# Seven-product groups that add up in one PSUM bank, the last product put off, and the third gate chunk by seven

## The chip, the cores and the metric

The kernel runs on one core of a Trainium2 chip. The metric is the time of one launch on the device in microseconds. The engines are TensorE (PE, matmuls; PEld are its weight loads), VectorE (DVE), ScalarE (ACT), GpSimd (POOL) and SyncE (SP), which issues the weight loads from HBM.

## The reference

A decoder trunk of two layers in float32 with 512 tokens and width 1024. Each layer is a half-step FFN, a mixer and a second half-step FFN; the first mixer is gated linear attention (GLA), the second is stick-breaking attention.

```python
def swiglu(h, w_gate, w_up, w_down):
    return (jax.nn.silu(h @ w_gate) * (h @ w_up)) @ w_down        # hidden width 2816

# GLA: chunks of 64, 4 heads, a decay by channel
log_a = jax.nn.log_sigmoid(gk_lr @ w_gk2 + b_gk) / 16
state = exp(b_last) * state + einsum(k * exp(b_last - b), v)      # b = cumsum(log_a)
o = rmsnorm(o, o_norm) * jax.nn.silu(g)

# stick-breaking: 16 heads of 64, blocks of 128 queries, mask: key before query
sp = where(mask, softplus(z), 0)
rem = cumsum(sp, reverse=True) - sp
weights = where(mask, exp(log_sigmoid(z) - rem), 0)

for i in range(2):
    x = x + 0.5 * swiglu(rmsnorm(x, ffn1_norm[i]), ...)
    x = x + mixer_i(rmsnorm(x, mix_norm[i]))
    x = x + 0.5 * swiglu(rmsnorm(x, ffn2_norm[i]), ...)
return rmsnorm(x, final_norm)
```

## The kernel before

Everything stays on chip but the weights. The residual is eight tiles `xs` of 128 features by 512 tokens. Each float32 operand is cut into a high and a low part (ACT writes the high one, L135 for weights, and DVE the rest, L136), and each product is three matmuls: high by high, low by high, high by low.

**FFN.** The hidden width is cut into 11 chunks of 256 columns, in six groups (`GROUPS`). Gate and up of a chunk are computed either as two features of 128 columns by `feat` (24 matmuls of 512 tokens each, PSUM tile `ps_f`, L64), or by `seven`: one 2×2 block product in the Strassen–Winograd form, seven products of 12 matmuls of 256 columns (L545) in place of eight, with sums of weight blocks (`s12`, `s34`) and of input blocks (`t_half`) on one side and additions of the results on the other. The ups go by `seven` from chunk 2 on, the gates from chunk 3 on (`SEVEN = 3`). The gated hidden tiles (high `hh`, low `hl`) of a group then go into the downs: one `down` accumulates `ps_d` over a group's tiles for some output features and adds into `xs` (L310).

**A group of seven before.** It uses three banks `w`, `z` and `q`, each in two halves. Four products fill or add on in the left halves, three have a half for themselves; five additions on DVE (`add`, L556, and L600) and two copies on ACT (`u2` at L580, `c5` at L587) put the two output tiles `o0` and `o1` together. For a gate, `left` (L560) applies Silu to the half that comes straight from PSUM, and `rest` (L566) applies it in place to what was added in SBUF; for an up the same two multiply by the gate. `rest` also keeps its Silu instruction in `st["silu"]`.

**Order.** Entries (a `feat`, a `down`, half a `seven`) stand in one queue, `feed`. It cuts weights up to three entries ahead and issues loads up to six ahead; raw weights have two buffers, cut weights four. What an engine executes in which order is set by a scheduler of the framework, which works from dependences and its own estimate of durations, and not by the source alone; `tc.issue_after(i)` adds only that an instruction does not come before `i`.

**Activation tables.** ACT holds one set of function tables at a time; ACT_TABLE_LOAD brings another. GLA and stick-breaking need Exp and Ln in turn. Before each of them the kernel asks for the one set that holds both, behind the last Silu it knows of:

```python
def exp_ln_tables(after):                      # L443, called with st["silu"]
    with tc.issue_after(after):
        st["tab"] = nc.scalar.preload_act_table_set("natural_log_exp_and_others").ins

def act(o, i, fn, **kw):                       # L447: every Exp and Ln of the mixers
    with tc.issue_after(st["tab"]):
        st["last"] = nc.scalar.activation(o, i, fn, **kw).ins
```

The last FFN does the same for a set with Sqrt (L716). Where an activation needs a set that is not the loaded one, the compiler puts a load ahead of it. `act` is what L450 is in the rows of the profile (L452 in the changed kernel).

**Stick-breaking.** Sixteen heads run as eight pairs. For each block of queries ACT makes the logits' parts `l` and `r` from PSUM (L1201, L1207), then Exp and Ln of `l` (L450), DVE adds, PE sums along the keys (`ps_T`), and ACT takes Exp of that for the weights `wt`. The projections of later heads run on PE in between.

Of the kernel before, what the change touches and what calls it, by code (L numbers as in the profile page):

```python
# [19 lines left out]
P = 128  # L20
# [12 lines left out]
def decoder(ctx: ExitStack, tc: tile.TileContext, a: dict, out: bass.AP):  # L33
# [257 lines left out]

                feed.q.append(Entry([u], body))

    def down(w, r0, nf, hs, part, nxt):

        nd = KD // nf
        src = w[r0 : r0 + nf * P, part * nd * P : (part + 1) * nd * P]
        ch = Chunk(src.rearrange("(f p) c -> p f c", p=P), nf, nd * P)
        ch.few = True

        def body(W):
            (wh, wl), = W
            for m in range(nd):
                ps = psum("ps_d")
                s = slice(m * P, (m + 1) * P)
                for f in range(nf):
                    mm3(ps, wh[:, f, s], wl[:, f, s], hs[f][0], hs[f][1], f == 0, f == nf - 1)
                k = part * nd + m
                x = like(xs[k], 4)
                nc.vector.scalar_tensor_tensor(  # L310
                    out=x, in0=back_by(ps, 4), scalar=0.5, in1=x, op0=ALU.mult, op1=ALU.add
                )
                if nxt is not None:
                    nxt(k)
                yield

        feed.q.append(Entry([(ch, lambda t: t, nf, nd * P)], body))
# [135 lines left out]
    class FFN:  # L453
# [4 lines left out]


        GROUPS = ((0, 2), (2, 4), (4, 6), (6, 8), (8, 9), (9, 11))  # L460
        NORMED, SEVEN = 6, 3
        SEVEN_UP = (2, 3, 4, 5, 6, 7, 8, 9, 10)

        def __init__(self, wg, wu, wd, gi, nxt, first=False, last=False):
            self.gi, self.normed, self.first = gi, False, first
            self.evac_g_, self.evac_u_ = self.evac_g, lambda ps: self.evac_u(ps, 0)
            if first:
                self.NORMED = 8
            self.defer, self.gates = [], []
            self.lead = []  # L470
            self.hs = [[] for _ in self.GROUPS]
            base, downs = len(feed.q), []
            self.base = base
            self.sums_by = 10**6
            for group, (c0, c1) in enumerate(self.GROUPS):
                slots, put = 2 * (c1 - c0), 0
                for i in range(slots):
                    c, f = c0 + i // 2, i % 2
                    if f == 0:
                        g, u = Chunk(cols(wg, c * 256, 256), KD, 256), Chunk(cols(wu, c * 256, 256), KD, 256)  # L480
                    d = self.defer if i == 0 and c == 0 else None
                    f_ = f
                    if first and c == 0:

                        g, u = (Chunk(cols(w, f * P, P), KD, P) for w in (wg, wu))
                        self.lead += [g, u]
                        f_ = 0
                    if c >= self.SEVEN:
                        if f == 0:
                            self.seven(g)  # L490
                    elif c not in self.SEVEN_UP:
                        feat(g, f_, self.evac_g, defer=self.defer if first and i == 1 else d, o=quads, m=four)
                    elif f == 0:
                        feat(g, 0, self.evac_g, o=quads, m=four), feat(g, 1, self.evac_g, o=quads, m=four)
                    if c not in self.SEVEN_UP:
                        feat(u, f_, lambda ps, h=group: self.evac_u(ps, h), defer=d, o=quads, m=four)
                    elif f == 1:
                        while c < self.SEVEN and put < len(downs) // 2:
                            down(*downs[put])
                            put += 1  # L500
                        self.sums_by = min(self.sums_by, len(feed.q) - base)
                        self.seven(u, group)

                    while c >= self.SEVEN and put < len(downs) * (i + 1) // slots:
                        down(*downs[put])
                        put += 1
                for x in downs[put:]:
                    down(*x)
                n = 2 * (c1 - c0)
                end = group + 1 == len(self.GROUPS)  # L510
                downs = [(wd, c0 * 256, n, self.hs[group], part, nxt if end else None) for part in range(n)]
            self.count = len(feed.q) - base
            if last:
                back_tok(wd, c0 * 256, n, self.hs[group], nxt)
            else:
                for x in downs:
                    down(*x)
            self.total = len(feed.q) - base

        def seven(self, ch, group=None):  # L520
# [43 lines left out]
            def rest(o, c):  # L564
# [4 lines left out]
                nc.vector.tensor_tensor(out=o[:, c:T], in0=o[:, c:T], in1=self.gates.pop(0)[:, c:T], op=ALU.mult)  # L569
                self.close(o, group)  # L570

            def body_1(W):
                ax, s = W

                v["w"], v["z"], v["q"] = psum("ps_w"), psum("ps_z"), psum("ps_q")
                w, z, q = (v[n][:, 0:H] for n in "wzq")
                v["o"] = self.tp.tile([P, T], F32, tag="t", name="o0")
                prod(w, ax, 0, half(0, 0))
                v["u2"] = part("u2")
                nc.scalar.copy(v["u2"], w)  # L580
                yield
                prod(z, s, 4, lambda j: self.t_half(1, j))
                add(v["u2"], z, v["u2"])
                yield
                prod(q, s, 0, lambda j: self.t_half(0, j))
                v["c5"] = part("c5")
                nc.scalar.copy(v["c5"], q)  # L587
                yield
                prod(w, ax, 4, half(4, 0), first=False)
                left(v["o"], w)  # L590
                yield

            def body_2(W):
                s, a22 = W
                q, y = v["q"][:, 0:H], v["z"][:, H:T]
                o0, o1 = v["o"], self.tp.tile([P, T], F32, tag="t", name="o1")
                prod(y, s, 0, lambda j: self.t_half(2, j))
                u3 = o1[:, 0:H]
                add(u3, y, v["u2"])
                nc.vector.tensor_tensor(out=o1[:, H:T], in0=u3, in1=v["c5"], op=ALU.add)  # L600
                yield
                prod(q, s, 4, half(4, 1), first=False)
                add(o0[:, H:T], q, v["u2"])
                rest(o0, H)
                yield
                o = v["w"][:, H:T]
                prod(o, a22, 0, lambda j: self.t_half(3, j))
                add(o1[:, 0:H], o, u3)
                rest(o1, 0)
                yield  # L610


            feed.q.append(Entry([(ch, lambda t: t[:, :, 0:P], KD, P), (ch, sums_12, KD, P)], body_1))
            feed.q.append(Entry([(ch, sums_34, KD, P), (ch, lambda t: t[:, 4:8, P:], 4, P)], body_2))

        def t_half(self, i, j):

# [71 lines left out]
        def run(self, between=None):  # L689
            with tc.tile_pool(name="hp", bufs=8, reuse_waits="tile") as self.hp, tc.tile_pool(  # L690
                name="tp", bufs=5, reuse_waits="tile"
            ) as self.tp:
                st["few"] = self.hp
                new_norm()

                if self.first:
                    with tc.manual_schedule():
                        feed.entries(1)
                        stats_b(turned=True)
                        flush(self.defer)  # L700
                else:
                    two_halves(stats_a)
                    stats_b(turned=True)
                    flush(self.defer)
                done = feed.pos - self.base
                for job, n in ((self.normed_input, self.NORMED - done), (self.sums, self.sums_by - self.NORMED)):
                    todo = list(job())
                    for i in range(n):
                        for piece in todo[i * len(todo) // n : (i + 1) * len(todo) // n]:
                            piece()  # L710
                        feed.entries(1)
                    self.normed = True
                    st["h"], st["l"] = zip(*self.n)
                feed.entries(self.count - self.sums_by)
                if between is not None:
                    with tc.issue_after(st["silu"]):  # L716
                        nc.scalar.preload_act_table_set("sqrt_and_others")
                    feed.q[feed.pos].split()
                    between(self.tp)
                feed.entries(self.total - self.count)  # L720
# [844 lines left out]
```

## Time and profile before

| | |
|---|---|
| median of 3 runs | 1797.32 us (1796.83 to 1797.62) |
| profiled execution, its own time | 1798.32 us |
| its span; mean granted clock of TensorE | 1796.5 us; 0.997 |
| PE, DVE, ACT busy | 1771.0, 1450.4, 906.9 us |
| read from HBM | 175.17 MB, 99 GB/s over the span |
| ACT_TABLE_LOAD in the program | 6: at L1395, L445 (twice), L674 (twice), L717 |
| first FFN; GLA; stick-breaking loop | to about 340 us; 340 to 560; 1250.62 to 1412.17 |

The page counts as busy the time in which an engine executes; the granted clock is 1 at full speed. In rows of the chain and of the timeline the first number is the start in us from the span's start and the second the time of the row's instructions together. In square brackets stands how long the engine had sat idle, and which instruction ended that. In groups, `| 28.6, 421 |` is busy us in all and mean ns of one. In rows of windows come the length, then for PE, PEld, DVE, ACT and POOL the busy time with its instructions, then PEclk, DMA share and GB/s.

### The profile page before, as it was taken

The page shows a single profiled execution, that of the slowest core. Times are in us where ns is not written, and L with a number is a line of the kernel's source. Part 1 is how long each engine was busy: PE and PEld are TensorE (multiplying, and loading weights), DVE is VectorE, ACT ScalarE, POOL GpSimd, SP SyncE. Part 2 cuts the span into 40 slices and gives each one's busy share as a digit, 9 for nine tenths or more (in the row PEclk, how much of TensorE's full clock was granted, in tenths as well). Part 3 has the DMA queues.
Part 4 walks back from the last instruction along what each step waited for, and adds up shares of the span by engine and source line. Part 5 has one row for each costly group of instructions (what it writes and reads, how often), then busy time and mean ns, then how long its engine had stood idle before and what let it go on. Part 6 is the DMA issues. An engine that isn't in the chain of part 4 may idle for free.

```text
span 1796.5 us, 30288 instructions
## 1 busy us (share of the span) xinstructions
PE 1771.0 (99%) x12502; PEld 1622.2 (90%) x12502; DVE 1450.4 (81%) x2371; ACT 906.9 (50%) x1428; POOL 9.6 (1%) x23
## 2 busy tenths in 40 slices
PE   9999999999999999999999999999999999999998
PEld 7899999888988899999989999998877888999997
DVE  7988887787868988878898888786777579888785
ACT  6544445455645444444554444454777544544444
POOL 0000000100000000000000000000000000000000
PEclk9999999999999999999999999999999999999999
DMA  6243333321222333333333333322222223333321
GB/s 212 71 133 114 106 118 103 96 72 57 87 71 94 117 106 106 106 113 100 107 111 101 106 106 118 106 83 83 59 71 71 71 94 118 106 106 111 125 83 71
DMA packets 177614, 179.19 MB, mean 100 GB/s; under 512 B 4098, under 2 KB 167988, under 8 KB 177476
## 3 DMA queue, kind: packets, MB, share of 16 engines
q1 hardware_dynamic: 176224, 175.13, 30.4%
q8 instruction: 98, 1.61, 0.4%
q0 software_dynamic: 576, 1.05, 0.2%
q10 hardware_dynamic: 676, 1.07, 0.2%
q14 instruction: 40, 0.33, 0.1%
HBM read 175.17 MB, written 2.10 MB: 99 GB/s over the span
## 4 chain that ended last, share of the span: by engine, by line
PE 84%; DVE 9%; ACT 3%; DMA 3%; issue 1%; SPq 0%; DVEq 0%; ACTq 0%
PE ps_d L64 24%; PE ps_w L545 15%; PE ps_f L64 13%; PE ps_z L545 10%; PE ps_q L545 10%; PE ps_t L64 4%; PE ps_b L64 4%; DVE wl L136 2%; DMA raw<-in_ffn_w_up_dram 2%; DVE l L1211 1%; PE ps_bt L64 1%; ACT wh L135 1%; PE ps_z L1167 1%; DVE r L1219 1%; DMA raw<-in_sb_w_in_dram 1%
## 5 line engine op out<-in xcount | busy, mean ns | idle before, releaser
L136 DVE TENSOR_TENSOR wl<-raw,wh 128x1024 fp32r<-128x1024 f32 x242 | 259.4, 1073 | 72.2 <-ACT wh L135 71.6
L135 ACT CAST wh<-raw 128x1024 fp32r<-128x1024 f32 (+1 forms) x242 | 223.9, 927 | 149.4 <-PE ps_f L64 53.1
L64 PE MATMUL ps_d<-hh,wh 128*128 128x512 f32 x672 | 254.9, 379 | 0.0
L64 PE MATMUL ps_d<-hh,wl 128*128 128x512 f32 x672 | 254.7, 379 | 0.0
L64 PE MATMUL ps_d<-hl,wh 128*128 128x512 f32 x672 | 254.7, 379 | 0.0
L135 ACT CAST wh<-s 128x1024 fp32r<-128x1024 f32 x136 | 142.2, 1046 | 117.0 <-PE ps_q L545 80.3
L136 DVE TENSOR_TENSOR wl<-s,wh 128x1024 fp32r<-128x1024 f32 x136 | 166.0, 1222 | 24.1 <-ACT wh L135 23.0
L64 PE MATMUL ps_f<-xh,wh 128*128 128x512 f32 x464 | 180.7, 390 | 0.3 <-DVE ol L1257 0.2
L64 PE MATMUL ps_f<-xh,wl 128*128 128x512 f32 x464 | 176.9, 381 | 0.5 <-DVE wl L1444 0.4
L64 PE MATMUL ps_f<-xl,wh 128*128 128x512 f32 x464 | 177.0, 381 | 0.0
L310 DVE SCALAR_TENSOR_TENSOR x<-ps_d,x 128x512 f32<-128x512 f32 x184 | 125.2, 689 | 60.9 <-PE ps_d L64 60.7
L545 PE MATMUL ps_z<-th,wh 128*128 128x256 f32 x544 | 150.1, 276 | 0.2 <-DVE u L556 0.2
L545 PE MATMUL ps_w<-nh,wl 128*128 128x256 f32 x544 | 149.6, 275 | 0.0
L545 PE MATMUL ps_w<-nl,wh 128*128 128x256 f32 x544 | 149.6, 275 | 0.0
L545 PE MATMUL ps_z<-th,wl 128*128 128x256 f32 x544 | 149.6, 275 | 0.0
L545 PE MATMUL ps_z<-tl,wh 128*128 128x256 f32 x544 | 149.6, 275 | 0.0
L545 PE MATMUL ps_w<-nh,wh 128*128 128x256 f32 x544 | 149.5, 275 | 0.0
L135 ACT CAST wh<-rawd 128x1024 fp32r<-128x1024 f32 x84 | 88.0, 1048 | 121.5 <-PE ps_d L64 103.2
L64 PEld LDWEIGHTS ps_d<-hl,wh 128*128 128x128 f32 x672 | 127.0, 189 | 18.0
L64 PEld LDWEIGHTS ps_d<-hh,wl 128*128 128x128 f32 x672 | 127.2, 189 | 16.5
L64 PEld LDWEIGHTS ps_d<-hh,wh 128*128 128x128 f32 x672 | 127.2, 189 | 16.5
L136 DVE TENSOR_TENSOR wl<-rawd,wh 128x1024 fp32r<-128x1024 f32 x84 | 102.8, 1224 | 34.5 <-ACT wh L135 34.1
(279 smaller groups left out, 4621.6 us busy)
## 6 DMA issues: line engine op xcount, KB each, us to landing
raw<-in_ffn_w_gate_dram SPq DMA_DIRECT2D x43, 1024.0 KB, 5.2
raw<-in_ffn_w_up_dram SPq DMA_DIRECT2D x43, 1024.0 KB, 5.2
rawd<-in_ffn_w_down_dram SPq DMA_DIRECT2D x84, 512.0 KB, 3.4
raw<-in_gla_w_in_dram SPq DMA_DIRECT2D x12, 1024.0 KB, 5.1
raw<-in_sb_w_in_dram SPq DMA_DIRECT2D x16, 512.0 KB, 3.8
raw<-in_gla_w_out_dram SPq DMA_DIRECT2D x4, 1024.0 KB, 5.0
raw<-in_sb_w_in_dram SPq DMA_DIRECT2D x4, 1024.0 KB, 5.2
raw<-in_sb_w_out_dram SPq DMA_DIRECT2D x4, 1024.0 KB, 4.9
```

The source lines that it names most:

```text
L64: st["pe"] = nc.tensor.matmul(ps, l, r, start=first, stop=last).ins
L135: nc.scalar.copy(h, r).ins,
L136: nc.vector.tensor_tensor(out=l, in0=r, in1=h.bitcast(F32), op=ALU.subtract).ins,
L310: nc.vector.scalar_tensor_tensor(out=x, in0=back_by(ps, 4), scalar=0.5, in1=x, op0=ALU.mult, op1=ALU.add)
L545: nc.tensor.matmul(pairs(o), l_, r_, start=first and j + n == 0, stop=j == 3 and n == 2, skip_group_check=True)
L1167: nc.tensor.matmul(o, l, r, start=first, stop=False, skip_group_check=True)
L1211: nc.vector.tensor_tensor_scan(out=l[:, c][:, ::-1], data0=r[:, c][:, ::-1], data1=l[:, c][:, ::-1], initial=0.0, op0=ALU.add, op1=ALU.add,)
L1219: nc.vector.tensor_tensor(out=r, in0=ps[:, 0:w], in1=l, op=ALU.subtract)
```

## The change

Four things are changed.

- **One bank.** ACT copies `w` into the bank `z` (from PSUM to PSUM), and the product that made `u2` is accumulated on top of it; ACT copies the sum out as `u2`. The product for the right half of `o1` is accumulated on top of that again, and the last product on top of that. DVE's additions fall from five to two per group, ACT's copies rise from two to three.
- **The last product is put off.** It becomes the function `fourth` in the list `self.later`, which `put_off` runs in the third step of the next group of seven, or ahead of a down that needs its tile, or before the last downs. Its `left` and `rest` (for a gate: the Silu of `o1`) go with it.
- **The third gate chunk by seven**: `SEVEN = 2`. Per FFN there are 18 groups of seven instead of 17 and two features fewer.
- **All downs of the first group ahead of it**: before, two stood behind the third chunk's gate features, and two behind its up; now all four stand ahead of the chunk's gate.

```diff
-    def down(w, r0, nf, hs, part, nxt):
+    def down(put_off, w, r0, nf, hs, part, nxt):
...
             (wh, wl), = W
+            if len(hs) < nf:
+                put_off()
...
-        NORMED, SEVEN = 6, 3
+        NORMED, SEVEN = 6, 2
...
                     if c >= self.SEVEN:
                         if f == 0:
+                            while c == self.SEVEN and put < len(downs):
+                                down(*downs[put])
+                                put += 1
+                            self.sums_by = min(self.sums_by, len(feed.q) - base)
                             self.seven(g)
...
                     elif f == 1:
-                        while c < self.SEVEN and put < len(downs) // 2:
-                            down(*downs[put])
-                            put += 1
-                        self.sums_by = min(self.sums_by, len(feed.q) - base)
                         self.seven(u, group)
...
                 prod(w, ax, 0, half(0, 0))
-                v["u2"] = part("u2")
-                nc.scalar.copy(v["u2"], w)
-                yield
-                prod(z, s, 4, lambda j: self.t_half(1, j))
-                add(v["u2"], z, v["u2"])
+                nc.scalar.copy(z, w)
                 yield
                 prod(q, s, 0, lambda j: self.t_half(0, j))
                 v["c5"] = part("c5")
                 nc.scalar.copy(v["c5"], q)
                 yield
+                self.put_off()
+                prod(z, s, 4, lambda j: self.t_half(1, j), first=False)
+                v["u2"] = part("u2")
+                nc.scalar.copy(v["u2"], z)
+                yield
                 prod(w, ax, 4, half(4, 0), first=False)
                 left(v["o"], w)
...
-                prod(y, s, 0, lambda j: self.t_half(2, j))
-                u3 = o1[:, 0:H]
-                add(u3, y, v["u2"])
-                nc.vector.tensor_tensor(out=o1[:, H:T], in0=u3, in1=v["c5"], op=ALU.add)
-                yield
                 prod(q, s, 4, half(4, 1), first=False)
                 add(o0[:, H:T], q, v["u2"])
                 rest(o0, H)
                 yield
-                o = v["w"][:, H:T]
-                prod(o, a22, 0, lambda j: self.t_half(3, j))
-                add(o1[:, 0:H], o, u3)
-                rest(o1, 0)
+                prod(z, s, 0, lambda j: self.t_half(2, j), first=False)
+                o1 = self.tp.tile([P, T], F32, tag="t", name="o1")
+                add(o1[:, H:T], z, v["c5"])
                 yield
 
+                def fourth():
+                    prod(z, a22, 0, lambda j: self.t_half(3, j), first=False)
+                    left(o1, z)
+                    rest(o1, H)
+
+                self.later.append(fourth)
...
+        def put_off(self):
+            while self.later:
+                self.later.pop()()
```

How the instructions stand on the engines at three places follows; a name's number tells one tile from another and differs between the kernels. Lines 445, 450, 560, 566 and 580 of before are lines 447, 452, 562, 568 and 592 of the changed kernel; its line 583 is the new copy.

ACT at the end of the first FFN, before (`o0`, `o1` are the last gate chunk's halves, `u2` and `c5` copies in the last group of seven, `rawd` weights of downs):

```order
L566 ACTIVATE o0_3291<-o0_3291 128x256
L135 CAST wh_3364<-raw_3119 128x512
L580 COPY u2_3435<-ps_w_3419 128x256
L566 ACTIVATE o1_3370<-o1_3370 128x512
L445 ACT_TABLE_LOAD
L587 COPY c5_3462<-ps_q_3421 128x256
L135 CAST wh_3477<-rawd_3286 128x1024
```

The same place now:

```order
L568 ACTIVATE o0_3318<-o0_3318 128x256
L568 ACTIVATE o1_3441<-o1_3441 128x256
L583 COPY ps_z_3450<-ps_w_3449 128x256
L447 ACT_TABLE_LOAD
L587 COPY c5_3478<-ps_q_3451 128x256
L135 CAST wh_3409<-raw_3151 128x512
L562 ACT_TABLE_LOAD
L562 ACTIVATE o1_3441<-ps_z_3316 128x256
L592 COPY u2_3506<-ps_z_3450 128x256
```

The Silu of `o1` was one operation of 512 columns ahead of the load; now its right half (L568) stands ahead of the load, and its left half (L562, from `ps_z`) behind it, with one more load directly ahead of it.

ACT at the start of one head pair of stick-breaking, before:

```order
L1188 COPY ps_z_14254<-ps_z_14254 128x1
L1201 ACTIVATE l_14289<-ps_z_14250 128x512
L1207 ACTIVATE r_14288<-ps_z_14250 128x512
L450 ACTIVATE l_14289<-l_14289 128x512
L450 ACTIVATE wt_14301<-ps_T_14296 128x512
L450 ACTIVATE l_14289<-l_14289 128x512
L1201 ACTIVATE l_14323<-ps_z_14252 128x512
L1207 ACTIVATE r_14322<-ps_z_14252 128x512
L450 ACTIVATE l_14323<-l_14323 128x512
L1201 ACTIVATE l_14357<-ps_z_14254 128x256
L450 ACTIVATE l_14323<-l_14323 128x512
L450 ACTIVATE wt_14336<-ps_T_14331 128x512
```

The same place now:

```order
L1198 COPY ps_z_14152<-ps_z_14152 128x1
L1211 ACTIVATE l_14187<-ps_z_14148 128x512
L1217 ACTIVATE r_14186<-ps_z_14148 128x512
L452 ACTIVATE l_14187<-l_14187 128x512
L452 ACTIVATE wt_14199<-ps_T_14194 128x512
L452 ACT_TABLE_LOAD
L452 ACTIVATE l_14187<-l_14187 128x512
L1211 ACTIVATE l_14220<-ps_z_14150 128x512
L1217 ACTIVATE r_14219<-ps_z_14150 128x512
L452 ACT_TABLE_LOAD
L452 ACTIVATE l_14220<-l_14220 128x512
L1211 ACTIVATE l_14255<-ps_z_14152 128x256
```

The activations are the same; loads of table sets stand between them.

PE in the third FFN behind the last up feature of chunk 1, before (`ps_f_10124` is that feature, `ps_f_10167` the first gate feature of chunk 2):

```order
L64 MATMUL ps_f_10124<-nh_10030,wl_10040 128x512
L64 MATMUL ps_f_10124<-nl_10031,wh_10039 128x512
L64 MATMUL ps_f_10167<-nh_9873,wh_10081 128x512
L64 MATMUL ps_f_10167<-nh_9873,wl_10082 128x512
L64 MATMUL ps_f_10167<-nl_9874,wh_10081 128x512
```

The same place now (`ps_f_10212` is that feature, `ps_d` the downs of the first group; their hidden tiles are 9951, 10055, 10161 and, made from `ps_f_10212`, 10239 with its low part 10240):

```order
L64 MATMUL ps_f_10212<-nl_10119,wh_10127 128x512
L64 MATMUL ps_d_10255<-hh_9951,wh_10169 128x512
...
L64 MATMUL ps_d_10255<-hh_10161,wh_10169 128x512
L64 MATMUL ps_d_10255<-hh_10161,wl_10170 128x512
L64 MATMUL ps_d_10255<-hl_10162,wh_10169 128x512
L64 MATMUL ps_d_10255<-hh_10239,wh_10169 128x512
L64 MATMUL ps_d_10255<-hh_10239,wl_10170 128x512
L64 MATMUL ps_d_10269<-hh_9951,wh_10169 128x512
L64 MATMUL ps_d_10269<-hh_9951,wl_10170 128x512
L64 MATMUL ps_d_10255<-hl_10240,wh_10169 128x512
```

The first down follows the feature directly, and its fourth hidden tile is the one that this feature makes.

More of the change, by code (lines that the diff above doesn't have):

```diff
@@ L469, in __init__ @@
             self.defer, self.gates = [], []
-            self.lead = []
+            self.lead, self.later = [], []
             self.hs = [[] for _ in self.GROUPS]
@@ L510, in __init__ @@
                 end = group + 1 == len(self.GROUPS)
-                downs = [(wd, c0 * 256, n, self.hs[group], part, nxt if end else None) for part in range(n)]
+                downs = [(self.put_off, wd, c0 * 256, n, self.hs[group], part, nxt if end else None) for part in range(n)]
             self.count = len(feed.q) - base
@@ L573, in body_1 @@
                 ax, s = W
-                v["w"], v["z"], v["q"] = psum("ps_w"), psum("ps_z"), psum("ps_q")
-                w, z, q = (v[n][:, 0:H] for n in "wzq")
+                v["w"], v["z"], v["q"] = (psum(n)[:, 0:H] for n in ("ps_w", "ps_z", "ps_q"))
+                w, z, q = (v[n] for n in "wzq")
                 v["o"] = self.tp.tile([P, T], F32, tag="t", name="o0")
                 prod(w, ax, 0, half(0, 0))
-                v["u2"] = part("u2")
-                nc.scalar.copy(v["u2"], w)
-                yield
-                prod(z, s, 4, lambda j: self.t_half(1, j))
-                add(v["u2"], z, v["u2"])
+                nc.scalar.copy(z, w)
                 yield
@@ L594, in body_2 @@
                 s, a22 = W
-                q, y = v["q"][:, 0:H], v["z"][:, H:T]
-                o0, o1 = v["o"], self.tp.tile([P, T], F32, tag="t", name="o1")
-                prod(y, s, 0, lambda j: self.t_half(2, j))
-                u3 = o1[:, 0:H]
-                add(u3, y, v["u2"])
-                nc.vector.tensor_tensor(out=o1[:, H:T], in0=u3, in1=v["c5"], op=ALU.add)
-                yield
+                q, z = v["q"], v["z"]
+                o0 = v["o"]
                 prod(q, s, 4, half(4, 1), first=False)
@@ L714, in run @@
                 feed.entries(self.count - self.sums_by)
+                self.put_off()
                 if between is not None:
```

## The prediction

> **What bounds the kernel now.** I read the page first (busy times, then the chain that ended last), then the chain row by row.
>
> ```profile
> PE 1771.0 (99%) x12502; PEld 1622.2 (90%) x12502; DVE 1450.4 (81%) x2371; ACT 906.9 (50%) x1428; POOL 9.6 (1%) x23
> PE 84%; DVE 9%; ACT 3%; DMA 3%; issue 1%; SPq 0%; DVEq 0%; ACTq 0%
> 96.02 5.18 PE ps_d L64 x24
> 102.54 1.34 PE ps_z L545 x12
> 110.71 5.18 PE ps_d L64 x24
> 125.27 5.18 PE ps_d L64 x24
> 904.60 41.54 PE ps_f L64 x192
> 946.14 10.36 PE ps_d L64 x48
> ```
>
> TensorE (PE) is busy for 99% of the span and is 84% of the chain. Inside an FFN it has no gap: from 110.71 to 125.27 stands one down (5.18) and one seven-product group (9.38), 14.56 us with nothing between. There, work taken off VectorE (DVE) buys nothing; only matmuls taken away do. ScalarE (ACT) is busy half the time on average, but that average hides the attention stages.
>
> **Term 1, the matmuls: −3.9 us.** Third gate chunk: 48 matmuls of 512 columns (10.36 us) become 84 of 256. From the rows above, 12 of these take 9.38/7 = 1.34 us, so 9.38 in all: 0.98 us less per FFN, 3.9 over four.
>
> **Term 2, additions and copies: 0.**
>
> ```profile
> L556 DVE TENSOR_TENSOR u<-ps_z,u 128x256 f32<-128x256 f32 x68 | 28.6, 421 | 10.1 <-PE ps_z L545 10.0
> L580 ACT COPY u<-ps_w 128x256 f32<-128x256 f32 x68 | 25.4, 374 | 20.3 <-PE ps_w L545 19.8
> ```
>
> Per group three DVE additions of 0.42 us go and one ACT copy of 0.37 us comes; a gate's second half takes its Silu in two operations of 256 columns instead of one of 512. Neither engine bounds an FFN, so 0. The new round trip, copy w to z and only then go on adding in z, costs PE nothing while the q product and the put-off one (2.68 us) stand between; without them it would be 0.37 us and up to one 1.05 us cast ahead of the copy in ACT's queue, per group.
>
> **Term 3, the downs moved forward: +5.** All four downs of the first group now follow the last up-matmul of chunk 1; two gate features of 5.18 us used to lie between. In the third FFN (the 946.14 row above starts the downs):
>
> ```profile
> 938.46 0.69 DVE L681 TENSOR_TENSOR t<-ps_f,t 128x512 f32<-128x512 f32 x1
> 939.18 0.62 ACT L631 CAST hh<-t 128x512 fp32r<-128x512 f32 x1 [2.06 <-DVE t L681]
> 940.80 0.69 DVE L632 TENSOR_TENSOR hl<-t,hh 128x512 fp32r<-128x512 f32 x1
> ...
> rawd<-in_ffn_w_down_dram SPq DMA_DIRECT2D x84, 512.0 KB, 3.4
> ```
>
> The up feature ends at 946.14 − 10.36 = 935.78. The first down reads three older tiles for 9 × 0.216 = 1.94 us, to 937.7, and then needs the new hh, ready at 939.8: PE waits 2.1 us. The new hl follows between 940.5 (at once behind hh) and 941.5 (as in the row), four products (0.9 us) later in PE's order: up to 0.8 more; I take 2.3 in all. By the same tiles I get 1.6 us in the fourth FFN and under 1 together in the first two. Queued behind this wait are all four downs and then the gate's seven, for which the feed has cut weights meanwhile. The downs' own loads (3.4 us to landing, last row) move ahead of the gate's in SP's queue too, but go out up to six entries early, at 5 us or more each: 0. At the end of an FFN the last put-off product stands directly before the last downs, with no down to cover it: 0.4 us, three times. Removed: about 1 us of small stalls at the old place. Together near +5, between 0 and +14 (the upper end if five sevens in a row also starve on weights by 1 us in each FFN). Terms 1 to 3 come to +1.
>
> **Term 4, the activation tables: this decides.** The order shows what the diff hides. The preload of the table set with Exp and Ln waits for `st["silu"]`, which is set by `rest`. In the put-off product, `left` (another Silu, from PSUM) comes from the last product and `rest` from an earlier one, so ACT executes rest, preload, then left. That needs the Silu set back, which throws the preloaded set out. The later Exp and Ln then no longer find a set with both, and each change from one to the other gets a load of its own: the program has 132 ACT_TABLE_LOAD instead of 6, of which 31 stand in the GLA and 91 in stick-breaking (10 to 12 for each of eight head pairs). Such loads now:
>
> ```profile
> L445 ACT ACT_TABLE_LOAD  x2: 1283/1283/1283, 307.8 to 1187.2; - x2
> 306.55 0.37 ACT L580 COPY u<-ps_w 128x256 f32<-128x256 f32 x1 [0.67 <-PE ps_w L545]
> 307.19 0.63 ACT L566 ACTIVATE o<-o 128x512 f32<-128x512 f32 x1 [0.27 <-DVE o L556]
> 307.84 1.28 ACT L445 ACT_TABLE_LOAD   x1
> 309.28 0.37 ACT L587 COPY c<-ps_q 128x256 f32<-128x256 f32 x1 [0.16 <-PE ps_q L545]
> 579.72 1.28 ACT L674 ACT_TABLE_LOAD   x1
> 581.01 0.63 ACT L674 ACTIVATE t<-t 128x512 f32<-128x512 f32 x1
> ```
>
> A load takes 1.283 us. It starts when the operation before it ends (307.82), and the next one starts when it ends (581.01); two activations otherwise overlap by about 0.1. So it costs ACT 1.28 + 0.13 = 1.41 us.
>
> *Stick-breaking.* The eight pairs run from 1250.62 to 1412.17; first the whole loop, then five steady pairs:
>
> ```profile
> 1250.62:1412.17 161.55, 154.95 (x1070) 129.14 (x1071) 123.33 (x188) 128.23 (x265) 0.00 (x0) 1.00 0.20 63
> 1291.84:1315.70 23.86, 21.70 (x138) 17.16 (x134) 16.34 (x25) 17.77 (x36) 0.00 (x0) 1.00 0.31 92
> ...
> 1377.80:1398.20 20.40, 18.99 (x132) 15.27 (x130) 15.27 (x23) 16.30 (x34) 0.00 (x0) 1.00 0.17 53
> sum 106.36, PE 101.79 PEld 82.86 DVE 80.73 ACT 83.80 POOL 0.00; mean PE 20.36 PEld 16.57 DVE 16.15 ACT 16.76 POOL 0.00
> L450 ACT ACTIVATE l<-l x96: 399/632/730, 1252.6 to 1411.5; 128x512 f32<-128x512 f32 x64, 128x256 f32<-128x256 f32 x32
> L450 ACT ACTIVATE wt<-ps_T x48: 370/590/718, 1266.3 to 1425.1; 128x512 f32<-128x512 f32 x32, 128x256 f32<-128x256 f32 x16
> ACT l L1201 <- PE ps_z L1167: 9.6, 8, 1.6
> ACT wt L450 <- PE ps_T L1232: 8.3, 7, 2.1
> ```
>
> A pair takes 106.36/5 = 21.27 us with ACT busy for 16.76. Twelve loads add 12 × 1.41 = 16.9: ACT then needs 33.7 us and becomes the bound. The floor is a fully packed ACT: 91 × 1.41 = 128 us less all its idle time in the loop, 161.55 − 128.23 = 33: +95. The ceiling is nothing absorbed, +128. I take +122: two handshakes remain in which ACT waits for PE whatever its load, the logits at the start of a pair (9.6/8 = 1.2 us in the waits) and the transposed sums ahead of the last weights (8.3/7 = 1.2, and I allow 2.6 because half-steps of projections stand ahead of them on PE). That gives 33.7 + 1.2 + 2.6 = 37.5 per pair, 16.2 more than now; by 7.5 such pairs (the loop's 161.55 over 21.27, the first and last being partly covered) 122.
>
> *The clock.* PE now gets gaps of some 5 us three times per pair. The trace has one place where PE is mostly idle for 2.1 us out of 4:
>
> ```profile
> 506.00:508.00 2.00, 0.74 (x89) 0.66 (x78) 0.75 (x2) 0.94 (x3) 0.00 (x0) 1.00 0.04 8
> 508.00:510.00 2.00, 1.18 (x49) 1.07 (x49) 0.50 (x2) 0.00 (x0) 0.00 (x0) 0.93 0.03 8
> 510.00:512.00 2.00, 2.00 (x6) 1.61 (x5) 1.79 (x9) 0.00 (x0) 0.00 (x0) 0.50 0.00 0
> 512.00:514.00 2.00, 2.00 (x8) 1.61 (x8) 0.26 (x2) 0.08 (x1) 0.00 (x0) 0.72 0.00 0
> ```
>
> Column PEclk (third from the end) falls to 0.50 and recovers: (1 − 0.93 + 1 − 0.50 + 1 − 0.72) × 2 = 1.7 us of PE work lost. Three times in eight pairs that is 41 us on PE; PE has 37.5 − 20.4 = 17 us free per pair, so only what falls where ACT waits for PE counts. I take 16, between 0 and 32. The Trainium skill ("TensorE: Matmul & The Clock Gate", "🔬 Part 1: The HAM clock gate (the "warmup" mystery)") has the array at half speed after an idle window of about 3.4 us; the 0.50 agrees, and by that rule every such gap would be hit, which is the upper end.
>
> *GLA.* 31 × 1.41 = 43.7 us of loads meet an ACT with much idle time:
>
> ```profile
> 340.00:560.00 220.00, 214.31 (x2074) 191.17 (x2073) 166.42 (x340) 114.62 (x195) 4.61 (x10) 0.98 0.23 75
> 366.86 2.18 ACT L450 ACTIVATE la<-la 128x512 f32<-128x512 f32 x4
> 371.53 1.80 ACT L450 ACTIVATE la<-la 128x512 f32<-128x512 f32 x3
> 375.74 0.63 ACT L450 ACTIVATE eb<-b 128x512 f32<-128x512 f32 x1 [2.40 <-DVE b L864]
> 392.83 0.85 PE L905 MATMUL ps_S<-e 128*32 128x64 f32 x31
> 539.82 0.63 ACT L450 ACTIVATE y<-vv 128x512 f32<-128x512 f32 x1 [2.25 <-DVE vv L1015]
> PE ps_b L64 <- DVE on L1029: 0.4, 1, 0.4
> ```
>
> Seven loads stand between the first decay logits (366.86) and eb (375.74); the one before eb hides in its 2.40 us wait, six delay the decay sums and with them ps_S at 392.83: 6 × 1.41 = 8. At the end six loads stand on the way of the last state and the last norm (539.82), for whose result PE already waits 0.4 us: another 8. Between, some +2. I take +18, between +8 (the head alone) and +44 (nothing absorbed).
>
> **Sum.** 122 + 16 + 18 + 1 = +157. The profiled execution took 1798.32, 1.0 above the median 1797.32, so against the median: 1797.3 + 157 = **1954 us**. Lower end 1797 + 95 + 8 − 4 = 1896, upper 1797 + 128 + 32 + 44 + 10 = 2011.
>
> The Trainium skill ("ScalarE: Activation LUTs", "What ACT_TABLE_LOAD costs") gives the same 1283 ns, but adds about 1380 ns of drain, 2.66 us per change of set; the rows at 581.01 and 309.28 show no such drain behind a load.
>
> **Rivals.** (a) *Each change of set also drains the engine*, at 1.3 us more than the load. For it: the rows above show only isolated loads, none with dependent activations on both sides. Against: 581.01 follows its load at once. Price: 12 × 1.3 = 15.6 more per pair, 7.5 pairs: +117, 1954 + 117 = about 2070. By the Trainium skill's page just named this would be the regular case. Chance 0.05.
>
> (b) *The loads are mostly absorbed*: PE's handshakes move into the time that ACT loads, the clock holds, GLA swallows all but the head. the sum of lower ends, 1896. For it: 33 us of idle ACT time in the loop. Against: each load stands directly before an operation that DVE or PE awaits. Chance 0.05.
>
> (c) *The other side: the loads cost nothing*, because the Silu from PSUM and the preloaded set turn out not to displace one another in the executed program, or the loads are dropped. Then only terms 1 to 3 are left: with the entry to the downs covered, 1797.3 − 3.9 = 1793.4, faster; with +5 for it, 1798, no change. It decides if the trace after has six loads. For it: nothing in the profile; six loads in the order of before stand in its trace at six places, and so I expect the 132. Chance 0.05, of which 0.03 faster and 0.02 the same.
>
> (d) *The clock takes over*: PE at half speed through the whole loop needs 2 × 20.36 = 40.7 us per pair, more than ACT's 33.7, and with the same handshakes a pair takes 44.5: 7.5 × 23.2 = 174, and 1797.3 + 174 + 18 + 1 = 1990. For it: three gaps per pair. Against: 512–514, where 2 us of work bring the clock back to 0.72. Chance 0.05.
>
> **How the numbers follow.** Forecast 0.80. About 0.2% (3.6 us) is the least that a measurement of this kernel tells from no change. Range: the ends 1896 and 2011, widened by that bound, 1892 to 2015; it takes in (d) and most of (b) and leaves out (a), (c) and about a tenth of the forecast's own spread, some 0.19 in all. Faster 0.03, same 0.02, slower 0.95.
>
> **What would show it.** Right: ACT_TABLE_LOAD on the line of `act` (L452) about 122 times, 91 of them inside the loop; a pair takes 36 to 39 us with ACT 33 to 34 busy and PE near 20 at full clock; the chain of waits runs through ACT there; the FFNs together change by less than 4 us. Wrong: loads of another number or length, pairs below 33 us, or an FFN that is longer by more than 5 us, which would mean that the downs' entry or the feed decides too. The number would also be wrong if the order of ACT's work were poor in a way that the sum above does not see: an operation held behind a load while PE waits for it in several places per pair.

## The result, and the profile after

The changed kernel takes 1955.95 us, the one before 1797.47 beside it: a ratio of 1.0877, with a 95% interval of 1.0859 to 1.0896, so 158 us slower. The forecast was 1954 us. (A ratio with its interval is an estimate of its own and need not be the exact quotient of the two medians.) The page of the changed kernel, busy times and chain:

```profile
PE 1823.8 (93%) x12646; PEld 1660.3 (85%) x12646; DVE 1406.9 (72%) x2235; ACT 1107.0 (57%) x1682; POOL 9.6 (0%) x23
PE 70%; ACT 16%; DVE 10%; DMA 2%; issue 1%; ACTq 0%; SPq 0%; DVEq 0%
```

ACT is busy 200 us longer and now holds 16% of the chain, where it held 3%. The group of the loads, by their line (durations in ns, then first and last start):

```profile
L452 ACT ACT_TABLE_LOAD  x122: 1283/1283/1283, 369.0 to 1568.3; - x122
```

The stick-breaking loop, from the first pair's start to the end of the last Ln, and five steady pairs (the same five as shown of before: first, last and their sum):

```profile
1282.48:1567.77 285.29, 197.71 (x1081) 159.83 (x1081) 129.34 (x189) 250.81 (x355) 0.00 (x0) 0.83 0.11 36
1349.98:1390.92 40.94, 27.64 (x138) 21.19 (x135) 17.18 (x26) 34.23 (x48) 0.00 (x0) 0.79 0.20 61
...
1502.85:1539.87 37.02, 24.23 (x132) 18.61 (x130) 16.09 (x23) 32.87 (x47) 0.00 (x0) 0.80 0.05 12
sum 189.89, PE 128.82 PEld 102.05 DVE 84.47 ACT 163.23 POOL 0.00; mean PE 25.77 PEld 20.41 DVE 16.89 ACT 32.65 POOL 0.00
```

A pair takes 189.89/5 = 37.98 us with ACT busy for 32.65; DVE's work is unchanged, and TensorE's granted clock is 0.83 in the loop. The head of one pair on ACT (timeline) shows the swaps one by one:

```profile
1398.24 0.63 ACT L452 ACTIVATE l<-l 128x512 f32<-128x512 f32 x1
1398.78 0.36 ACT L1211 ACTIVATE l<-ps_z 128x256 f32<-128x256 f32 x1
1399.16 1.28 ACT L452 ACT_TABLE_LOAD   x1
1400.46 0.63 ACT L452 ACTIVATE l<-l 128x512 f32<-128x512 f32 x1
1401.10 1.28 ACT L452 ACT_TABLE_LOAD   x1
1402.40 0.60 ACT L452 ACTIVATE wt<-ps_T 128x512 f32<-128x512 f32 x1
```

There is no idle time in it: Exp, a logit part from PSUM (L1211), load, Ln, load, Exp. Where the time went, by stages that begin and end at matmuls which both kernels have (us, from one profiled execution of each, so 2 or 3 us mean little):

| stage | before | after | difference | tables kept (below) |
|---|---|---|---|---|
| start to the decay logits of GLA | 364.5 | 366.6 | +2.1 | 366.8 |
| to the first group of seven of the second FFN | 263.9 | 291.8 | +27.9 | 266.5 |
| to the first logits of stick-breaking | 619.4 | 621.6 | +2.2 | 622.3 |
| to the last output product of stick-breaking | 181.4 | 304.6 | +123.2 | 184.5 |
| to the last matmul | 359.4 | 362.6 | +3.1 | 361.0 |

Almost all of it is in the two mixers, whose code the diff does not touch.

### The profile page after: what moved, and what is told of

It is laid out like the page before. It is cut to its first block, busy times and chain, and to the rows that moved or that the text cites. A ratio compares the mean times of both kernels' runs of the same rounds, so it can differ in the third digit from the quotient of the medians.

```text
span 1954.9 us, 30524 instructions
## 1 busy us (share of the span) xinstructions
PE 1823.8 (93%) x12646; PEld 1660.3 (85%) x12646; DVE 1406.9 (72%) x2235; ACT 1107.0 (57%) x1682; POOL 9.6 (0%) x23
## 4 chain that ended last, share of the span: by engine, by line
PE 70%; ACT 16%; DVE 10%; DMA 2%; issue 1%; ACTq 0%; SPq 0%; DVEq 0%
PE ps_d L64 20%; PE ps_z L547 14%; PE ps_q L547 10%; PE ps_w L547 10%; ACT L452 7%; PE ps_f L64 5%; PE ps_b L64 3%; ACT l L452 3%; DVE wl L136 2%; PE ps_t L64 2%; ACT wh L135 2%; DMA rawd<-in_ffn_w_down_dram 1%; ACT l L1211 1%; PE ps_bt L64 1%; DVE ts L650 1%
## 5 line engine op out<-in xcount | busy, mean ns | idle before, releaser
L136 DVE TENSOR_TENSOR wl<-raw,wh 128x1024 fp32r<-128x1024 f32 (+1 forms) x242 | 257.2, 1063 | 176.5 <-ACT wh L135 175.4
L547 PE MATMUL ps_z<-th,wh 128*128 128x256 f32 x864 | 238.3, 276 | 0.5 <-ACT ps_z L583 0.5
L547 PE MATMUL ps_z<-tl,wh 128*128 128x256 f32 x864 | 237.7, 275 | 0.0
L547 PE MATMUL ps_z<-th,wl 128*128 128x256 f32 x864 | 237.7, 275 | 0.0
L136 DVE TENSOR_TENSOR wl<-s,wh 128x1024 fp32r<-128x1024 f32 x144 | 175.7, 1220 | 30.2 <-ACT wh L135 28.1
L64 PE MATMUL ps_f<-xh,wh 128*128 128x512 f32 x464 | 189.6, 409 | 0.1
L547 PEld LDWEIGHTS ps_z<-th,wh 128*128 128x128 f32 x864 | 165.9, 192 | 1.3 <-ACT ps_z L583 0.7
L547 PEld LDWEIGHTS ps_z<-th,wl 128*128 128x128 f32 x864 | 165.9, 192 | 0.1
L547 PEld LDWEIGHTS ps_z<-tl,wh 128*128 128x128 f32 x864 | 165.9, 192 | 0.0
L452 ACT ACT_TABLE_LOAD x122 | 156.5, 1283 | 4.4 <-DVE vv L1025 2.2
L547 PE MATMUL ps_w<-nh,wh 128*128 128x256 f32 x576 | 158.6, 275 | 0.0
```

Of the source, the lines that this page charges most:

```text
L64: st["pe"] = nc.tensor.matmul(ps, l, r, start=first, stop=last).ins
L136: nc.vector.tensor_tensor(out=l, in0=r, in1=h.bitcast(F32), op=ALU.subtract).ins,
L547: nc.tensor.matmul(pairs(o), l_, r_, start=first and j + n == 0, stop=j == 3 and n == 2, skip_group_check=True)
```

## The experiments

**The loads are nearly the whole loss.** Two runs test it from both sides. The first is the changed kernel with the preload behind the put-off Silu:

```diff
-                    nc.scalar.activation(o[:, 0:H], w, AF.Silu)
+                    st["left"] = nc.scalar.activation(o[:, 0:H], w, AF.Silu).ins
...
                     rest(o1, H)
+                    if group is None:
+                        st["silu"] = st["left"]
```

> The changed kernel, but the preload of the Exp and Ln set (and of the Sqrt set) waits for the put-off left Silu too, so that the program has 6 loads of table sets again; all else as changed. Theory (the table loads are the whole loss, the rest is worth about nothing): 1798 us, between 1793 and 1802. Rival (the moved downs, the put-off product or the feed cost a part of the 158 us by themselves): above 1806 us.

Measured: 1809.9 us against 1799.56 beside it, ratio 1.0053 (1.0040 to 1.0065). The table loads cost 0.0877 − 0.0053 of the time before, 148 us. But 9.5 us (7 to 12) are left. That is the rival's condition: the rest of the change costs something by itself, and the theory's "rest is worth about nothing" falls.

The second is the kernel before, with the loss of the set and nothing else:

```diff
-                    st["silu"] = nc.scalar.activation(o[:, c:T], o[:, c:T], AF.Silu).ins
+                    i_ = nc.scalar.activation(o[:, c:T], o[:, c:T], AF.Silu).ins
+                    if c:
+                        st["silu"] = i_
```

> The kernel before with one edit: the preload of the Exp and Ln set waits for the Silu of the first half of the last gate chunk only, so that the second half's Silu throws the set out; 132 loads of table sets, nothing else of the change. Theory: 1797 + 158 = 1955 us, between 1945 and 1962. Rival (the loads cost that much only together with the other parts of the change, which move the order of the work): below 1935 us.

Measured: 1950.34 us, ratio 1.0837 (1.0810 to 1.0863), +151 us. One line about an order on ACT costs the kernel before what the loads cost the changed one: the 148 above lie within the interval. Its stick-breaking loop takes 285.23 us, against 285.29 in the changed kernel. Its four executions stand in two groups, though, 1945.23 and 1945.86 us at a mean granted clock of 0.971, 1954.82 and 1955.91 at 0.964; 151 is the middle of them. What that says of GLA follows with the prediction.

**GLA's part.** The changed kernel with `exp_ln_tables(st["left"])`, that is with its set kept, for stick-breaking alone:

> The changed kernel with the set lost ahead of GLA only and kept for stick-breaking; 31 loads in GLA, none in the stick-breaking loop. Theory: the kernel with tables kept plus 29 to 31 us, since the stretch from the first to the second L445 and L674 loads grew by 30.3 us in the trace; 1828 us. Rival of the prediction's own size for GLA (18 us): 1816 us. Rival (all of the loads are absorbed where ACT has idle time, the 30 us come from the FFN's end): within 5 us of the kernel with tables kept.

Measured: 1832.99 us, 1.0186 (1.0169 to 1.0202): 0.0133 over the kernel with tables kept, 24 us. That lies between the 30 that I had read from the trace and the 18 of the prediction; the 30 was taken between two table loads, whose places on ACT differ between the kernels, and by the stages above GLA costs 291.8 − 266.5 = 25 us more than with tables kept.

**Half the loop.** GLA with its set, stick-breaking without, and one preload ahead of the fifth pair:

```diff
                 for p, n in enumerate(self.FEED + ((1, 1, 1),)):
+                    if p == 4:
+                        exp_ln_tables(st["last"])
```

> The changed kernel with the set kept for GLA, lost ahead of stick-breaking, and loaded again by one preload ahead of the fifth of the eight head pairs; 47 loads in the first half of the loop. Theory (each pair pays for its own loads): the kernel with tables kept plus half of the loop's 124 us and the 3 us ahead of it: +60 to +68, 1862 us; pairs after the preload near 21 us at full clock. Rival (a slow part of the loop puts the later pairs out of step, or the clock stays low): +80 us or more.

Measured: 1868.97 us, 1.0383 (1.0367 to 1.0399): 0.0330 over the kernel with tables kept, 59 us, a little under what was expected and half of the loop's 120 (184.5 to 304.6). The windows of the two halves of its loop:

```profile
1257.99:1405.60 147.61, 104.19 (x534) 83.32 (x534) 69.07 (x99) 131.04 (x183) 0.00 (x0) 0.82 0.12 36
1405.60:1487.50 81.90, 79.34 (x567) 66.54 (x568) 61.56 (x95) 64.61 (x134) 0.00 (x0) 1.00 0.18 59
```

Four pairs with loads take 147.61 us, 36.9 each, at clock 0.82; the pairs behind the preload start at 1405.60, 1426.72, 1447.09 and 1467.46, 20.6 us apart, at full clock. Each pair pays for its own loads and nothing is carried over.

**What the clock costs** was to be told by added products with zeros (12 of 512 columns, 2.6 us) in the half-steps ahead of PE's two longest gaps; the sums are unchanged:

```diff
                 for k in ks:
+                    if k == ks[-1] and st.get("warm"):
+                        for _ in range(12):
+                            mm(o(ps), wh[:, k], m(st["zero"]), False, False)
                     mm3(ps, wh[:, k], wl[:, k], st["h"][k], st["l"][k], k == 0, k == KD - 1, o, m)
```

> The changed kernel with its table loads, and in each head pair of stick-breaking two half-steps of projections get 2.6 us of added products with zeros, just ahead of the two places where PE waited 4.3 to 5.5 us for the weights; results are the same, PE has more to do where it waits anyway. It is not a clean edit: the scheduler moves some ACT work and the loop has 93 loads instead of 91 (2.7 us). Theory A (the clock is what PE's gaps cost on the path: ACT's two waits for PE grew by 7.6 and 1.3 us in the loop): granted clock in the loop above 0.95 instead of 0.83, and the loop 5 to 9 us shorter but for the two loads, so 279 to 283 us instead of 285.5. Theory B (ACT's queue alone sets the loop): clock above 0.95 too, but the loop 285 to 291 us. Rival (the added products land on the path): above 295 us.

Measured: 1966.05 us, 1.0917 (1.0902 to 1.0932). Its loop, and what PE waited for in it (us in all, times, longest):

```profile
1280.47:1575.79 295.32, 212.61 (x1189) 173.23 (x1189) 129.75 (x191) 255.40 (x358) 0.00 (x0) 0.86 0.11 34
PE ps_T L1245 <- ACT wt L455: 39.0, 11, 5.8
PE ps_oT L1260 <- ACT wt L455: 20.0, 5, 8.6
```

This fails as a test. The edit reaches only the projections that `feat` computes: the trace has 108 added matmuls in nine blocks, and not two blocks in each of the eight pairs. The gaps ahead of `ps_T` shrink (66.7 us in the changed kernel's loop) and others open ahead of `ps_oT` (9.0 there, 20.0 here); the clock rises only from 0.83 to 0.86, and the loop is longer. The condition of theories A and B, a clock above 0.95, was not met; the rival's, a loop above 295 us, just was.

**The 9.5 us that are left.** Four runs split them. The third chunk by seven and the moved downs, without the one bank and with nothing put off (the kernel before with `SEVEN = 2` and the downs' new place):

> The kernel before with only the third gate chunk by seven and all downs of the first group ahead of it; groups of seven with three banks and five additions, nothing put off. Theory (the entry to the downs costs 3 us, the saved matmuls bring 3.9): -1 us against before, between -3 and +2. Rival (the moved downs or five groups of seven in a row are what costs 10 us): +8 us or more.

Measured: 1802.45 against 1799.87, 1.0012 (1.0002 to 1.0021), +2.1 us: just past the theory's +2 and far from the rival's +8. If the 3.9 us of matmuls are saved as worked out, the moved downs cost about 6. The other half, one bank and the put-off product with the third chunk and the downs as before, tables kept:

> The changed kernel with tables kept, but the third gate chunk by features and the downs at their old places; so one bank, copies and the put-off product alone. Theory (the put-off product uncovers the last downs for 3.5 us and the copies into the bank cost PE 0.7; the rest of the 10 us is spread over small waits): +5 to +9 us against before. Rival (the put-off product is free where DVE is relieved): -1 to +2 us.

Measured: 1805.28, 1.0029 (1.0018 to 1.0039), +5.2 us, as the theory had it. The two halves add to 7.3, within the interval of the 9.5. What PE waits for in the kernel with tables kept shows at the last downs of the first FFN (timeline of PE, DVE and ACT):

```profile
321.30 1.22 DVE L136 TENSOR_TENSOR wl<-rawd,wh 128x1024 fp32r<-128x1024 f32 x1
321.82 0.38 PE L64 MATMUL ps_d<-hl,wh 128*128 128x512 f32 x1
322.43 0.42 DVE L564 TENSOR_TENSOR o<-ps_z,o 128x256 f32<-128x256 f32 x1
322.88 0.62 ACT L642 CAST hh<-o 128x512 fp32r<-128x512 f32 x1 [2.39 <-DVE o L564]
323.56 0.48 PE L64 MATMUL ps_d<-hh,wh 128*128 128x512 f32 x1 [1.36 <-ACT hh L642]
```

The put-off product is done, but its multiplication by the gate (L564) stands on DVE behind a cut of weights that started at 321.30; then comes the cast, and PE waits 1.36 us for the last hidden tile. So I took the last up group out of the putting off:

```diff
+                if group == len(self.GROUPS) - 1:
+                    fourth()
+                else:
+                    self.later.append(fourth)
```

> The changed kernel with tables kept (6 loads), and in addition the last up group of each FFN adds its last product at once instead of putting it off to just ahead of the last downs. Theory: in the run with tables kept PE waited for hh ahead of the last downs for 1.4, 0.3, 0.8 and 1.1 us; these 3.5 us go, and of the 10 us that the kernel with tables kept stands above the one before some 6 remain: +4 to +8 us against before. Rival (the waits only move, because DVE is late there anyway): +9 to +11 us.

Measured: 1808.39, 1.0051 (1.0037 to 1.0065), +9.2 us; the rival is right. The waits of PE in the kernel with tables kept (first row) and then, in a fence of its own, of this run:

```profile
PE ps_d L64 <- ACT hh L642: 5.1, 6, 1.4
```

```profile
PE ps_d L64 <- ACT hh L645: 2.7, 3, 1.1
PE ps_z L547 <- DVE o L558: 2.0, 8, 0.4
```

The waits for `hh` fall by 2.4 us and a new one of 2.0 appears: the last product now adds on in the bank `z` before DVE has read it. Then the entry was covered too, by an order of the products in the first down of each group:

```diff
+            both = part == 0 and nd == 2
+            if both:
+                products(0, range(nf - 1))
+                products(1, range(nf - 1))
             for m in range(nd):
-                ps = psum("ps_d")
...
+                products(m, (nf - 1,) if both else range(nf))
```

> The kernel of the run that does not put off the last up product, and in addition the first down of each group takes the three older hidden tiles for both of its outputs before the newest one. Theory (the waits for hh at the downs are the loss that is left in the FFNs): 2 to 3 us below that run. Rival (they are covered by something else that is late next, such as the weights of the group that follows): within 1 us of that run.

Measured: 1803.75, 1.0026 (1.0017 to 1.0035): 4.5 us below the run before it, where 2 to 3 were expected: more than the waits that were named.

**A kernel that is faster than both.** The same order of the products, put on the kernel with the third chunk alone:

> The kernel before with the third gate chunk by seven, all downs of the first group ahead of it, and the first down of each group taking its three older hidden tiles for both outputs before the newest one. In the run of the third chunk alone PE still waited 2.6 us for hh, 0.4 for hl and about 1 us more for weights at the downs. Theory: those 3 us go, 2 us or less below before: -3 to 0 us against before. Rival (as with the last up: the wait moves): +1 to +3 us.

Measured: 1796.88 against 1800.71, 0.9973 (0.9964 to 0.9983), −4.9 us, beyond the 3 that were expected at most. PE's waits at the downs in the run of the third chunk alone:

```profile
PE ps_d L64 <- ACT hh L631: 2.6, 3, 1.1
PE ps_d L64 <- DVE wl L136: 1.0, 1, 1.0
PE ps_d L64 <- DVE hl L632: 0.4, 2, 0.2
```

and with the entry covered:

```profile
PE ps_d L64 <- DVE wl L136: 0.9, 1, 0.9
PE ps_d L64 <- DVE hl L643: 0.2, 1, 0.2
```

The waits for `hh` are gone. They and the two others account for 2.9 us of the 7 between the two runs (+2.1 and −4.9); where the rest came from is not shown. Two more runs ask whether it holds and whose doing it is. The covered entry on the kernel before, without the third chunk:

> The kernel before with one edit: the first down of each group takes its three older hidden tiles for both outputs before the newest one; third gate chunk by features as before. Theory (PE does not wait for hh at the downs in the kernel before, so there is nothing to cover): -1.5 to +1.5 us against before. Rival (the interleaved downs themselves are what made the kernel with the third chunk and the covered entry 5 us faster): -4 us or less.

Measured: 1799.95 against 1800.10, 0.9996 (0.9987 to 1.0006): nothing, as there is no wait to cover. And the faster kernel again:

> The kernel with the third gate chunk by seven and the covered entry once more, to see whether it stands below the kernel before on another occasion: -3 to -6 us against before, if the last result holds; within 2 us, if that was a difference between occasions.

Measured: 1796.31 against 1800.10, 0.9977 (0.9968 to 0.9986), −4.1 us. The saving of the third chunk is real, 4 to 5 us (2.5 to 6.5 by the intervals) where 3.9 were worked out, once PE does not wait for `hh` at the downs that were moved.

## Why the prediction was right, and where not

The forecast of 1954 met 1955.95 for the right reason: the lost table set carries 148 of the 158 us. That it met within 2 us is luck, as its parts are off in both directions and cancel: loop and clock by −14 us, GLA by +6, terms 1 to 3 by +8.5. Of the signs that it named, the 122 loads, the 91 of them in stick-breaking and the 37.98 us of a pair came true; ACT is busy for 32.65 us of a pair, just under the 33 named, and the FFNs did not stay within 4 us.

- **The lost table set** (term 4). Shown: the loads are there as the order told (122 on L452, 31 in GLA, 91 in stick-breaking), they cost 148 us when taken out of the changed kernel and 151 when put into the one before, and pair for pair they cost the same. Rivals (a), (b) and (c) are out, and (d) too, with PE busy for 25.77 of a pair's 37.98 us. The trace also settles rival (a)'s drain: behind 121 of the 122 loads the next operation starts no more than 0.02 us after the load's end, and the operations around them keep their 0.60 to 0.63 us. The Trainium skill ("ScalarE: Activation LUTs", "What ACT_TABLE_LOAD costs") counts 1380 ns of drain with each change of set; this trace agrees with its 1283 ns and not with the drain.
- **The price of a load**, 1.41 us, was 4% too high: ACT's busy time in the loop grew by 250.81 − 128.23 = 122.6 us for the 90 loads in that window (the last of the 91 starts at 1568.26, behind its end), 1.36 each.
- **The loop's +122** measured +123.7 (285.29 − 161.55); a pair takes 37.98 us where 37.5 was worked out. The reasoning behind it, that ACT's idle time stays because handshakes with PE remain, holds: 33.3 us before, 285.29 − 250.81 = 34.5 after. The handshakes are these (ACT's waits in the changed kernel's loop):

```profile
ACT wt L452 <- PE ps_T L1242: 15.9, 8, 4.6
ACT l L1211 <- PE ps_z L1177: 10.9, 8, 2.9
```

- **The clock's +16** is the term that was mis-sized most. Loop and clock together were put at 138 and measured 124, and no run tells the two apart. The clock does fall as forecast, behind a gap of 4.7 us (timeline of PE in the changed kernel):

```profile
1397.96 0.38 PE L64 MATMUL ps_f<-xl,wh 128*128 128x512 f32 x1
1403.05 0.69 PE L1242 MATMUL ps_T<-ident,r 128*128 128x128 f32 x2 [4.71 <-ACT wt L452]
1403.39 0.78 PE L64 MATMUL ps_f<-xh,wh 128*128 128x512 f32 x1
1403.96 0.63 PE L64 MATMUL ps_f<-xh,wl 128*128 128x512 f32 x1
```

The 0.38 us of a matmul become 0.63 behind the gap. But ACT's two waits for PE grew only from 8.3 to 15.9 and from 9.6 to 10.9, 8.9 us together, and with other waits of ACT that vanished all its idle time grew by only 1.2. That makes the clock's part in the loop look small, but is no bound; how much it is stays open, since the run meant for it did not keep PE busy.

- **GLA's +18** measured 24 by the runs and 25 by the stages. What is missing is mostly the clock, which the prediction counted in the loop and put at nothing in GLA. These two waits of PE stand in GLA's tail in the changed kernel:

```profile
PE ps_kd L983 <- DVE kd L973: 5.4, 1, 5.4
PE ps_b L64 <- DVE on L1039: 3.0, 1, 3.0
```

The kernel before with the one changed line has the same 31 loads there and almost the same two waits, 5.5 and 3.0 us, but in its profiled execution PE kept more of its clock. The stage from the decay logits to the second FFN's first group of seven in the changed kernel, with tables kept, and in that run (length, PE busy, PEclk third from the end):

```profile
366.60:658.36 291.76, 267.50 (x2271) 234.57 (x2272) 216.94 (x413) 180.89 (x261) 0.00 (x0) 0.95 0.24 77
366.81:633.29 266.48, 257.71 (x2271) 228.28 (x2272) 216.00 (x413) 140.62 (x230) 0.00 (x0) 0.99 0.27 84
365.44:648.30 282.86, 259.46 (x2271) 228.50 (x2272) 214.53 (x411) 181.92 (x263) 0.00 (x0) 0.99 0.25 79
```

For the same 2271 matmuls PE is busy 9.8 us longer in the changed kernel than with tables kept, and only 1.8 in that run. With most of the clock kept, GLA is 282.86 − 263.89 = 19 us longer than before, and the +18 is about right for the loads alone; the changed kernel's stage is another 8.9 us longer, 8.0 of them in PE's busy time. By start times behind the decay logits the delay is, in that run against before, 6.4 us at the first state sums, 9.1 at the third `ps_kd`, 15.1 at the last and 18.7 at the last output product; in the changed kernel against tables kept 8.3 (36.6 against 28.3), 8.1, 17.8 and 25.6. So the head's +8 came out by a part of clock that it did not count (granted clock 0.91 over the head here, 1.00 in that run), and the tail's +8 is 9.6 with most of the clock and 17.5 without it. The two groups of that run's executions, 10 us apart at clocks of 0.971 and 0.964, are of the same size; where the slower two lost their clock was not profiled.

- **Terms 1 to 3, +1**, measured +9.5 (7 to 12). Term 1 fits the faster kernel (−3.9 worked out, −4.9 and −4.1 measured). Term 3 at +5 was about right: +2.1 against −3.9 makes 6. Term 2 with the put-off product was not: priced at 0 and three times 0.4, it is +5.2 (3 to 7). The step that failed took the engines' spare time for cover. On average DVE has it, but at the last downs the one operation that counts is queued behind a cut of weights of 1.22 us. Of the 5.2 us the listed waits of PE show about half; where the rest lies was not found.

## What to carry to other kernels

A table set that is loaded ahead stays only until the next function that needs another one: whoever moves an activation later must move every preload that was tied to an earlier one, and count the loads in the program, since the diff shows none of it. An engine that is busy for 50% of the whole span can become the bound of a stage, here by 12 loads of 1.3 us in a pair of 21 us; read such a cost from the stage. Where loads open gaps on TensorE, count its clock in every stage that it bounds, and not only in the one where the gaps are most. A saving of matmuls on a full TensorE arrived here only once the first consumer of the newest tile had other products to do until that tile was there.

## What was not expected of the hardware

A load of a table set costs hardly more than its own 1.283 us, 1.36 us of ACT's time, even when 91 of them alternate with short operations on both sides. TensorE's clock does not fall alike behind like gaps: over the 5 us behind the 3.0 us wait in GLA's tail it was 0.50 in the changed kernel (first row) and 1.00 in the kernel before with one changed line (second row):

```profile
570.22:575.22 5.00, 5.00 (x12) 4.01 (x13) 3.01 (x5) 1.22 (x2) 0.00 (x0) 0.50 0.01 3
564.22:569.22 5.00, 5.00 (x23) 4.32 (x24) 3.89 (x7) 1.77 (x3) 0.00 (x0) 1.00 0.00 0
```

Keeping TensorE busier ahead of some of its gaps did not keep its clock up: with nine blocks of about 2.6 us of added products the mean went from 0.83 to 0.86, and gaps opened in other places.
